# Log-sum-exp kernel: last half tiles with three TensorE-biased heads folded by GpSimd, and two tiles loaded whole

## The chip, the cores and the metric

One core of one Trainium2 chip. The metric is the device time of one execution in microseconds (us). A profile of one execution goes with each kernel; its span is some 2 us shorter than the time, because it runs from the first to the last instruction. Engines in the profile: PE is TensorE's matmuls, PEld its weight loads, DVE is VectorE, ACT ScalarE, POOL GpSimd, SP the engine that issues the loads.

## The reference, cut to what matters

```python
B, S, D, H = 8, 2048, 2048, 8
x_heads = x.reshape(B, S, H, D // H).transpose(0, 2, 1, 3) + bias[None, :, None, :]
x_tiled = np.repeat(x_heads, 2, axis=2)
mx = x_tiled.max(axis=-1, keepdims=True)
lse = mx.squeeze(-1) + np.log(np.exp(x_tiled - mx).sum(axis=-1))
```

For each row and each of 8 heads: the log of the sum over 256 columns of exp(x + bias), each result written twice. The 128 MB input is read once.

## The kernel before

The input comes in 64 tiles of 256 rows (2 MB: 128 partitions, 2 rows, 2048 columns). A head's sum is made in one of four ways:

- TensorE puts the bias in PSUM and adds x by a matmul with the identity ("biased head"); ScalarE takes the exp from PSUM and sums with its accumulator.
- ScalarE takes exp(x) in place and VectorE multiplies by exp(bias) and sums, in one custom instruction ("weighted sum").
- GpSimd adds the bias in SBUF (tiles 0 to 56).
- GpSimd multiplies exp(x) by exp(bias) and halves the head by additions to 32 columns, and VectorE sums these ("fold").

```python
PROMPT_F1 = dict(pe=2, acc=2, g0=8, late=False, fold=1)   # 2 biased heads, 5 weighted, 1 folded
PROMPT_F2 = dict(pe=2, acc=2, g0=8, late=False, fold=2)
SINGLE_F1 = dict(pe=1, acc=1, g0=8, late=False, fold=1)
TRIPLE = dict(pe=3, acc=3, g0=8, late=False, fold=0)
STAGES = [(0, (BULK,)), (54, (MIXED,)),          # whole tiles
    (57, (PROMPT_F1, PROMPT_F1)),                # half tiles from here on
    (62, (SINGLE_F1, SINGLE_F1)), (63, (PROMPT_F2, TRIPLE))]
# ... cut ... the main loop, for one piece (t, k0) of a tile:
            heads = add_x(m, t, k0, c0, c1, bias_here)        # TensorE: x of this half
            if c0 == 0:
                bias_there = put_bias(*next_units.pop(0))     # TensorE: bias of the next half
                keep_warm()                                   # TensorE: three idle matmuls into tp
                flush(for_pool)
            done = exp_inplace(t, ...)                        # ScalarE
            if c0 == 0:
                flush(for_pe)      # ScalarE: biased heads of the half before
            # ... cut ... VectorE: weighted sums
        # ... cut ... after a whole tile, two tiles after a batch's end:
        finish(fb)     # TensorE: four transposes into tp; ScalarE: one Ln of 32x1024 out of tp
```

In the profiles each engine starts its instructions in the order of the program: around tile 57 TensorE starts x of 57.0 at 285.11 us, the next bias at 287.12, the warm matmuls at 287.65, x of 57.1 at 289.09 and the transposes, which the program issues last of these, at 291.91. "Warm matmuls" multiply the identity by itself; nobody reads their result. "57.0" and "57.1" are the two halves of tile 57.

The softmax here doesn't subtract the row's maximum and nothing guards it: scores larger than these inputs give would overflow.

## Time and profile before

| | us |
|---|---|
| time, median of 3 runs | 325.56 (325.21 to 325.87) |
| span of the profiled run | 323.1 |
| half 62.1 lands / ScalarE starts on it | 312.38 / 312.45 |
| ends: GpSimd, ScalarE's sums, VectorE | 319.17, 319.43, 319.63 |

Three lines of the page: busy time and share of each engine, then TensorE's granted clock and the loads in 40 slices of the span, in tenths.

```profile
PE 270.3 (84%) x691; PEld 102.9 (32%) x691; DVE 283.9 (88%) x306; ACT 265.8 (82%) x426; POOL 287.7 (89%) x120
PEclk9979799979979996998997997997999999559998
DMA  8999999999999999999999999999999999999995
```

TensorE (PE), VectorE, ScalarE and GpSimd are each busy for over 80% of the time and the loads keep the DMA engines at eight or nine tenths until the last slice (419 GB/s over the span). No share tells what the end waits for; that is read from the last 36 us, as the prediction does. The two 5s in the clock row are the stretch from 273.6 to 290.6 us in which the clock records have TensorE at half clock; there an x matmul pair takes 2.08 us (at 285.11) and after it 1.02 (at 292.35).

### The profile page before, as it was taken

How to read it: one execution, taken by the hardware profiler on the slowest of the kernel's cores; microseconds unless marked ns; L12 is line 12 of the kernel's file. 1: busy time of each engine (PE TensorE's matmuls, PEld its weight loads, DVE VectorE, ACT ScalarE, POOL GpSimd, SP SyncE). 2: the span in 40 equal slices, each digit the busy share in tenths (PEclk: the TensorE clock that was granted, in tenths of full speed). 3: DMA queues.
4: the chain of work that ended last, by engine and by line, in shares of the span. 5: the costliest groups of instructions: out<-in, count | busy, mean ns of one | idle time of the engine just before them, and what ended most of it. 6: DMA issues, size and time to landing. Idle time of an engine off the chain costs nothing.

```text
span 323.1 us, 2398 instructions
## 1 busy us (share of the span) xinstructions
PE 270.3 (84%) x691; PEld 102.9 (32%) x691; DVE 283.9 (88%) x306; ACT 265.8 (82%) x426; POOL 287.7 (89%) x120
## 2 busy tenths in 40 slices
PE   5999999889978769977869886888997786599984
PEld 2333333333323223322323322333333232035442
DVE  1037779999999998999899899898999999999995
ACT  1148679889869976988888978889998998899995
POOL 6939998999999999999999999999999999858874
PEclk9979799979979996998997997997999999559998
DMA  8999999999999999999999999999999999999995
GB/s 311 457 402 454 450 400 439 450 402 446 438 414 446 432 418 443 430 422 447 422 426 441 422 434 442 404 426 430 432 422 431 430 428 425 416 422 421 419 401 170
DMA packets 8830, 135.42 MB, mean 419 GB/s; under 512 B 1041, under 2 KB 1425, under 8 KB 2417
## 3 DMA queue, kind: packets, MB, share of 16 engines
q1 hardware_dynamic: 8720, 135.27, 98.6%
q8 instruction: 5, 0.08, 0.1%
q14 instruction: 7, 0.06, 0.0%
q10 hardware_dynamic: 98, 0.01, 0.0%
HBM read 134.23 MB, written 1.05 MB: 419 GB/s over the span
## 4 chain that ended last, share of the span: by engine, by line
DMA 40%; POOL 18%; ACT 17%; PE 14%; DVE 9%; issue 0%; SPq 0%; DVEq 0%
DMA xb<-in_x_dram 40%; POOL xb L376 18%; ACT xb L382 11%; DVE R L401 6%; PE pair L326 5%; PE one_ps L326 3%; PE pair L267 3%; ACT xb L357 2%; PE one_ps L267 2%; DVE xb L417 2%; PE pair L219 1%; ACT xb L337 1%; DVE xb L394 1%; ACT res L471 1%; ACT xb L344 1%; DMA brow<-in_bias_dram 1%
## 5 line engine op out<-in xcount | busy, mean ns | idle before, releaser
L376 POOL TENSOR_TENSOR xb<-xb,b_rep 128x2048 f32<-128x2048 f32 x57 | 257.6, 4539 | 20.7 <-DMA xb<-in_x_dram 20.6
L401 DVE TENSOR_REDUCE R<-xb 128x14 f32<-128x3584 f32 (+1 forms) x56 | 214.5, 3830 | 1.9
L382 ACT ACTIVATE xb<-xb 128x2560 f32<-128x2560 f32 (+5 forms) x77 | 157.1, 2050 | 10.3 <-POOL xb L376 10.1
L326 PE MATMUL pair<-xb,ident 128*128 128x512 f32 x216 | 114.3, 656 | 0.0
L326 PE MATMUL one_ps<-xb,ident 128*128 128x512 f32 x108 | 67.5, 710 | 11.5 <-DMA xb<-in_x_dram 11.5
L344 ACT ACTIVATE xb<-pair 128x1024 f32<-128x1024 f32 x54 | 55.5, 1027 | 23.2 <-PE pair L326 23.0
L326 PEld LDWEIGHTS pair<-xb,ident 128*128 128x128 f32 x216 | 46.2, 214 | 61.3 <-issue 61.3
L394 DVE TENSOR_TENSOR xb<-xb,w_ps 128x512 f32<-128x512 f32 x54 | 36.7, 681 | 26.2 <-ACT xb L382 26.2
L337 ACT ACTIVATE xb<-one_ps 128x256 f32<-128x256 f32 x108 | 40.0, 380 | 6.6 <-PE one_ps L326 6.6
L267 PEld LDWEIGHTS <-ones 3*128 3x128 bf16 (+1 forms) x192 | 16.9, 95 | 80.8 <-issue 71.4
L267 PE MATMUL one_ps<-b,ones 3*128 3x512 bf16 x49 | 18.6, 380 | 25.4 <-ACT xb L337 25.3
L267 PE MATMUL pair<-b,ones 3*128 3x512 bf16 x98 | 29.0, 375 | 0.0
L326 PEld LDWEIGHTS one_ps<-xb,ident 128*128 128x128 f32 x108 | 17.2, 200 | 33.9 <-DMA xb<-in_x_dram 18.0
L302 PE MATMUL pair<-xb,ident 128*128 128x512 f32 (+1 forms) x36 | 21.7, 689 | 5.7 <-DMA xb<-in_x_dram 5.7
L417 DVE CUSTOM_DVE_ANT_0 xb<-xb,w_ps 128x256 f32<-128x256 f32 x61 | 22.4, 418 | 0.0
L337 ACT ACTIVATION_READ_ACCUMULATOR xb<-one_ps 128x1 f32 x108 | 22.3, 207 | 0.0
L441 POOL TENSOR_TENSOR xb<-xb 128x128 f32<-128x128 f32 (+3 forms) x39 | 13.8, 355 | 3.1
L433 POOL TENSOR_TENSOR xb<-xb,w_sb 128x256 f32<-128x256 f32 (+1 forms) x13 | 10.0, 771 | 5.2 <-ACT xb L382 4.5
L317 PE MATMUL tp<-ident 128*128 128x128 f32 x84 | 13.7, 302 | 0.0
L317 PEld LDWEIGHTS tp<-ident 128*128 128x128 f32 x84 | 11.1, 200 | 3.5 <-issue 3.0
L357 ACT ACTIVATE xb<-pair 128x256 f32<-128x256 f32 x33 | 11.9, 364 | 0.0
L417 DVE CUSTOM_DVE_ANT_0 xb<-xb,one_ps 128x256 f32<-128x256 f32 x27 | 10.6, 415 | 0.1
(42 smaller groups left out, 83.4 us busy)
## 6 DMA issues: line engine op xcount, KB each, us to landing
xb<-in_x_dram SPq DMA_DIRECT2D x20, 4096.0 KB, 21.5
xb<-in_x_dram SPq DMA_DIRECT2D x17, 2048.0 KB, 22.7
xb<-in_x_dram SPq DMA_DIRECT2D x12, 1024.0 KB, 22.7
xb<-in_x_dram SPq DMA_DIRECT2D x4, 256.0 KB, 13.2
out_dram<-res SPq DMA_DIRECT2D x1, 896.0 KB, 6.7
xb<-in_x_dram SPq DMA_DIRECT2D x2, 384.0 KB, 15.8
xb<-in_x_dram SPq DMA_DIRECT2D x2, 128.0 KB, 6.3
out_dram<-res_last SPq DMA_DIRECT2D x1, 128.0 KB, 1.7
```

The lines of the kernel that those rows point to most:

```text
L267: nc.tensor.matmul(p, lhsT=lhsT, rhs=each_row(b, h * Dh, Dh, K), start=i == 0, stop=False,)
L302: mm = nc.tensor.matmul(p, lhsT=ident, rhs=xts[t % NBUF][:, ka:kb, c : c + w], start=False, stop=True,)
L317: nc.tensor.matmul(tp[:, 0], lhsT=ident, rhs=ident, start=True, stop=True)
L326: mm = nc.tensor.matmul(p, lhsT=ident, rhs=xts[t % NBUF][:, :, h * Dh : (h + 1) * Dh], start=False, stop=True,)
L337: act = nc.scalar.activation(out=xts[t % NBUF][:, k, 0:Dh], in_=got[0][:, k * Dh : (k + 1) * Dh], func=ACT.Exp, accum_out=sums[:, k, 0:1],)
L344: act = nc.scalar.activation(out=xts[t % NBUF][:, :, Dh : m["pe"] * Dh].rearrange("p k (h j) -> p h k j", j=Dh), in_=got[-1].rearrange("p ...
L357: act = nc.scalar.activation(out=xts[t % NBUF][:, k, h * Dh : (h + 1) * Dh], in_=p, func=ACT.Exp, accum_out=sums[:, k, h : h + 1],)
L376: add = nc.gpsimd.tensor_tensor(out=v, in0=v, in1=each_row(b_rep, c - G0, D - c, k1 - k0), op=ALU.add)
L382: return on_x(t, nc.scalar.activation(out=v, in_=v, func=ACT.Exp), [after])
L394: mul = nc.vector.tensor_tensor(out=f, in0=f, in1=each_row(w_ps, m["pe"] * Dh - W0, n, k1 - k0), op=ALU.mult,)
L401: red = nc.vector.tensor_reduce(out=sums[:, k0:k1, h0:H], in_=v.rearrange("p k (h j) -> p k h j", j=Dh), op=ALU.add, axis=mybir.AxisListTy ...
L417: ttr = nc.vector.tensor_tensor_reduce(out=v, in0=v, in1=w, scale=1.0, scalar=0.0, op0=ALU.mult, op1=ALU.add, accum_out=dst,)
```

## The change

Its intent is to take work from VectorE, on which the chain ended, and to save two load instructions. Halves 62.0, 62.1 and 63.0 get three biased heads, of which ScalarE takes one exp from a pair of PSUM banks without summing ("biased exp" below); GpSimd folds all three, without a multiplication. Tiles 57 and 58 are loaded whole. The program gives a three-head unit both banks of a pair, and it puts the next bias after ScalarE's work of the half before, and no longer ahead of the warm matmuls.

```diff
+UNIT_LOADS = 59
-PROMPT_F2 = dict(pe=2, acc=2, g0=8, late=False, fold=2)
-SINGLE_F1 = dict(pe=1, acc=1, g0=8, late=False, fold=1)
+FOLDED = dict(pe=3, acc=0, g0=8, late=False, fold=0)
-    (62, (SINGLE_F1, SINGLE_F1)),
-    (63, (PROMPT_F2, TRIPLE)),
+    (62, (FOLDED, FOLDED)),
+    (63, (FOLDED, TRIPLE)),
-    [(0, 512), (1280, 2048), (512, 1280)],
+    [(0, 768), (1280, 2048), (768, 1280)],
@@ load
+        if t < UNIT_LOADS:
+            ins = nc.sync.dma_start(out=xts[t % NBUF], in_=rows_of(t))
@@ put_bias: a three-head unit starts on a whole pair of banks
+        if n > MM:
+            n_ps[0] += n_ps[0] % 2
@@ new
+    def exp_biased(t, k, n, heads):
+        act = nc.scalar.activation(out=xts[t % NBUF][:, k, 0 : n * Dh],
+            in_=pairs[bank // 2][:, 0 : n * Dh], func=ACT.Exp)
@@ fold: multiplies only heads that carry no bias yet
+        if h0 * Dh >= W1:
@@ main loop
+                    if m["acc"] == 0:
+                        done = exp_biased(t, k, m["pe"], heads)
+                        for_pool.append(fold(t, k, 0, m["pe"], sums, done))
+                        return
-                if next_units and not m["late"]:
-                    bias_there = put_bias(*next_units.pop(0))
-                if t > T_PROMPT and m["g0"] == H:
+                if t > T_PROMPT and m["g0"] == H and m["pe"] * Dh <= MM:
                     keep_warm()
-            if c0 == 0:
+            if c0 == 0 or t == T - 1 and k0 == 0:
                 flush(for_pe)
+            if c0 == 0 and next_units and not m["late"]:
+                bias_there = put_bias(*next_units.pop(0))
```

(Bookkeeping of bank users and of the fold's chain of dependencies is cut.)

More of the change, by code (lines that the diff above doesn't have):

```diff
@@ L166, in load @@
         after = last_uses[t - NBUF] if t >= NBUF else []
+        if t < UNIT_LOADS:
+            ins = nc.sync.dma_start(out=xts[t % NBUF], in_=rows_of(t))
+            on_x(t, ins, after)
+            for k0, _, c0, _ in pieces(t):
+                loads[t, k0, c0] = ins
+            return
         for k0, k1, c0, c1 in pieces(t):
@@ L244, with on_bank @@
     bank_users = [[], []]
-    def on_bank(i, ins):
-        for j, u in bank_users[i // 2]:
-            if j != i and u.ins.engine != ins.ins.engine:
+    def on_bank(i, ins, both=False):
+        pair = i // 2
+        i = None if both else i
+        for j, u in bank_users[pair]:
+            if None not in (i, j) and j != i and u.ins.engine != ins.ins.engine:
                 tc.declare_no_dep(ins.ins, u.ins, reason="another bank")
-        bank_users[i // 2].append((i, ins))
+        bank_users[pair].append((i, ins))
         return ins
@@ L313, in add_x @@
         return heads
+    def exp_biased(t, k, n, heads):
+        _, _, bank, _, mm = heads[-1]
+        act = nc.scalar.activation(
+            out=xts[t % NBUF][:, k, 0 : n * Dh],
+            in_=pairs[bank // 2][:, 0 : n * Dh],
+            func=ACT.Exp,
+        )
+        on_bank(bank, on_x(t, act, [mm]), both=True)
+        return act
     def keep_warm():
@@ L432, in fold @@
         v = xts[t % NBUF][:, k, h0 * Dh : h1 * Dh]
-        done = nc.gpsimd.tensor_tensor(
-            out=v, in0=v, in1=w_sb[:, h0 * Dh - W1 : h1 * Dh - W1], op=ALU.mult
-        )
-        on_x(t, done, [after])
+        done = after
+        if h0 * Dh >= W1:
+            mul = nc.gpsimd.tensor_tensor(
+                out=v, in0=v, in1=w_sb[:, h0 * Dh - W1 : h1 * Dh - W1], op=ALU.mult
+            )
+            done = on_x(t, mul, [done])
         v = v.rearrange("p (h j) -> p h j", j=Dh)
@@ L440, in fold @@
             n //= 2
-            done = nc.gpsimd.tensor_tensor(
+            add = nc.gpsimd.tensor_tensor(
                 out=v[:, :, 0:n], in0=v[:, :, 0:n], in1=v[:, :, n : 2 * n], op=ALU.add
             )
-            on_x(t, done, [])
+            done = on_x(t, add, [done])
         def add_up():
@@ L535, with pe_part @@
                 heads = add_x(m, t, k0, c0, c1, bias_here)
-                def pe_part(t=t, heads=heads, sums=sums):
+                def pe_part(t=t, m=m, k=k0, heads=heads, sums=sums):
+                    if m["acc"] == 0:
+                        done = exp_biased(t, k, m["pe"], heads)
+                        for_pool.append(fold(t, k, 0, m["pe"], sums, done))
+                        return
                     for k, h, bank, p, mm in heads:
```

## The prediction

> **What bounds the kernel now.** I read the page first, then the chain of waits from 286 us on, then the timeline of each engine there; the change touches nothing earlier. The program has 64 tiles of 2 MB; from tile 57 on each is worked on in halves ("57.0", "57.1"). For most of the span the loads bound it: the DMA row shows 9 in every slice but the first and last, 419 GB/s. From 287 us the chain is something else:
>
> ```profile
> 282.59 4.55 POOL xb L376
> 287.17 4.66 ACT xb L382 x3
> 291.82 0.72 ACT xb L357 x4
> 292.55 1.01 ACT res L471
> 293.56 1.38 ACT xb L382
> ...
> 309.53 0.71 ACT xb L357 x4
> 310.24 1.59 ACT xb L382
> 311.83 0.71 ACT xb L357 x4
> 312.54 1.60 ACT xb L382
> 314.16 0.42 DVE xb L417
> 320.11 0.38 ACT res_last L488
> ```
>
> The columns are start, length, engine and line. GpSimd's bias add of tile 56 ends at 287.14, and from there ScalarE works without a gap until the exp of half 62.1 ends at 314.14. Then VectorE takes over: 62.1's six weighted sums, 63.0's four, 63.1's five, at 0.34 each, then a fold's reduce, the transpose, Ln and the store. The timeline of the end:
>
> ```profile
> 312.38 0.70 PE L302 MATMUL pair<-xb,ident 128*128 128x256 f32 x2 [0.72 <-DMA xb<-in_x_dram]
> 312.45 1.68 ACT L382 ACTIVATE xb<-xb 128x1792 f32<-128x1792 f32 x1
> ...
> 317.51 1.66 POOL L441 TENSOR_TENSOR xb<-xb 128x256 f32<-128x256 f32 x3
> ...
> 319.25 0.18 ACT L357 ACTIVATION_READ_ACCUMULATOR xb<-pair 128x1 f32 x1
> ...
> 319.41 0.22 DVE L447 TENSOR_REDUCE R_last<-xb 128x2 f32<-128x64 f32 x1
> ```
>
> The reader is to see that half 62.1 lands at 312.38 and ScalarE gets to it at 312.45, so ScalarE has just caught up with the loads and has nothing in hand; and that all three tail engines end close together: GpSimd 319.17, ScalarE 319.43, VectorE 319.63. The rest (319.63 to 323.1) is fixed. So a delay of ScalarE after 287 us, or a later end of any one of the three, moves the time almost one for one.
>
> [...] 128x128 takes 457 ns, 128x256 730 ns, 2.13 ns per element. [...] the same 512-column x matmul pair takes 2.08 us at 285.11 and 1.02 us at 292.35, and the clock records give half clock from 273.6 to 290.7. [...]
>
> **The change part by part.**
>
> *Loads.* Tiles 57 and 58 come as one 2 MB load each. In the trace halves land 2.485 us apart and whole tiles 4.90, so two tiles save 2 x (4.97 - 4.90) = 0.15 us of loading: 62.1 lands at 312.23. But 57.0 is no longer there at 285.11; the tile lands whole at about 282.59 + 4.86 = 287.45. ScalarE doesn't mind, since it exps 57.0 at 288.9 and 58.0 at 293.5. TensorE does:
>
> ```profile
> 285.11 2.08 PE L302 MATMUL pair<-xb,ident 128*128 128x512 f32 x2
> 287.12 0.60 PE L284 MATMUL pair<-b,ones 3*128 3x512 bf16 x1
> 287.65 1.65 PE L317 MATMUL tp<-ident 128*128 128x128 f32 x6
> 289.09 1.80 PE L302 MATMUL pair<-xb,ident 128*128 128x512 f32 x2
> 290.82 0.38 PE L284 MATMUL pair<-b,ones 3*128 3x512 bf16 x1
> 291.14 0.94 PE L317 MATMUL tp<-ident 128*128 128x128 f32 x6
> 291.91 0.60 PE L461 MATMUL tp<-ident,R 128*32 128x128 f32 x4
> ```
>
> This queue is in order, and its last row is the transpose that ScalarE's Ln of the first seven batches (292.55, in the chain) waits for. In the changed program it still stands behind both halves of tile 57 (the order of the bias and the warm matmuls is swapped, which costs nothing by itself). From 287.45: x of 57.0 at half clock 2.0, warm matmuls 1.25, bias 0.35, weights and x of 57.1 at full clock 1.2, warm 0.75, bias 0.3, transposes 0.7: done at 294.0 against 292.5. ScalarE then stalls about 1.4 us in front of its Ln. [...]
>
> *ScalarE in the tail.* Back to back a 1536 exp takes a step of 1.37 and a 1792 exp 1.59, 0.21 per 256 columns; so 1280 takes 1.16, and 768 takes 0.73 (826 ns, overlapping by 0.1). A PSUM source costs the same (1024 columns, 1.03 us). Tiles 62 and 63.0 lose four one-head exps with their accumulator reads (0.355 each) and gain three 768 exps from PSUM, while the exps in place shrink by 512, 512 and 256 columns. The sum of ScalarE's work falls from 8.57 to 8.3 us: no lever either way.
>
> *VectorE.* Halves 62.0 and 62.1 go from six to five weighted sums, 63.0 from four to five: one less, -0.34; three reduces of 96 instead of 32, 32 and 64 elements give back about 0.2.
>
> *GpSimd.* It loses the multiplications (0.73, 0.73 and 1.27 us) and folds three heads of each of 62.0, 62.1, 63.0. At 2.13 ns per element 384, 192 and 96 elements take 1.00 + 0.59 + 0.39 us, plus two gaps of 0.08: 2.14 each, 6.43 for three, against 1.92 + 1.92 + 3.0 before. The sum is slightly smaller, but it starts later. Before, the fold of 62.0 began at 311.91, right after the exp of its last heads. Now it needs the exp of the biased heads of 62.0, and in the changed order that stands behind 62.0's other exp, 61.1's two heads and the exp of 62.1, which waits for its load.
>
> *The sum.* Let A be the start of the exp of 62.1. The biased exp of 62.0 ends at A + 1.16 + 0.72 + 0.10, GpSimd starts at A + 2.04 and ends its third fold at A + 8.47, and the last reduce (0.25) ends at A + 8.75. On the other engines: TensorE's bias and x for 63.0 need the pair that 62.0 had, about 2.0 us (bias 0.5, weights, 512 and 256 columns 1.45) after A + 1.98, so ScalarE's biased exp of 63.0 starts at A + 4.0 and ScalarE ends at A + 7.85; VectorE, held up by the reduce of 62.0's fold, comes out at A + 8.15. GpSimd ends last by some 0.3 us. Without the stall, A is 312.23 + 0.07 = 312.30 and the last reduce ends at 321.05, 1.42 later than 319.63. With a stall of 1.4, A is 310.15 + 1.4 + 1.16 + 0.71 = 313.42, and the end is 2.54 later. So the working gives 325.56 + 1.4 = 327.0 to 325.56 + 2.5 = 328.1. I choose 327.4: [...] a tuned change is more likely to have a delay that I overrate than one that I miss.
>
> **The rivals.**
>
> *It gains.* The intent is to drain VectorE, on which the chain ends. If VectorE alone set the end, and the biased exps came as promptly as before, one weighted sum less and loads 0.15 us earlier make 325.1. For it: VectorE is busy from 314.16 to the end. Against it: GpSimd and ScalarE end within 0.5 us of it, so they take its place at once.
>
> *Only the tail counts, no Ln stall.* If TensorE's clock rises early, or the transposes come sooner, the time is 327.0. [...]
>
> *The clock stays low longer.* With 57.0 late TensorE idles from 285.2 to 287.4; [...]
>
> *The early loads matter.* Fewer loads could shorten everything by 0.15 us. But ScalarE, not the loads, is the chain from 287 to 314; it is hidden.
>
> **Range and chances.** The rival with a gain and the worked sum with the stall span 325.1 to 328.1, the slow clock adds a tail above. The range is 325.4 to 328.9. All these lie within 2% (319.0 to 332.1): faster by over 2% would need 6.5 us from a tail of 36 us whose loads alone end at 317.6; slower by over 2% would need the slow clock and a second delay.
>
> **What would show it.** Right: an idle time of ScalarE of 0.6 to 1.5 us in front of L471's successor, ended by TensorE's transpose; three GpSimd folds of about 2.1 us each, back to back, the first starting near 314.3 to 315.5; a last reduce on VectorE that waits for GpSimd; a wait of about 0.5 us of ScalarE for TensorE before the biased exp of 63.0. Wrong: a fold of three heads well under 2 us, GpSimd done before VectorE, or ScalarE passing the Ln without a gap and starting 62.0 at 310.15 or earlier.

Gone are two other sizes of the stall: a smaller one, for an earlier rise of the clock, which was the 0.6 us in "0.6 to 1.5 us" (an estimate of the author without working), and a larger one, for a later rise, on which the part of the range above 328.1 rests; and with them what was said for and against these two clock rivals. For the larger one the trace gives a size: the half-clock stretch from 222.41 to 225.82 us lasts 3.41; were the one before the Ln longer by as much, TensorE would be behind by half of that, 1.7 us, the stall some 3.1 and the time some 329.8 (an estimate from these numbers).

## The result, and the profile after

The changed kernel takes 328.76 us (median of 4, 328.04 to 328.99) against 325.38 (median of 4) before. The ratio is 1.0098, 95% interval 1.0078 to 1.0118: slower by 1%, within the 2% of "same". A ratio here and below is the mean time of one kernel's fast runs over that of the other's fast runs of the same rounds, so not quite the ratio of the medians. Executions over 1.5% slower than the fastest of the same kernel are left out of the means.

The page of the changed kernel, busy times and clock row:

```profile
PE 267.4 (82%) x676; PEld 102.0 (31%) x676; DVE 284.6 (87%) x304; ACT 265.8 (82%) x421; POOL 287.6 (88%) x117
PEclk9989799979979987997999997997999997569997
```

GpSimd's and ScalarE's busy sums moved by 0.1 us or less and VectorE's by 0.7, while the span grew by 2.9. So hardly any work was added; it was moved and made to wait. The chain of waits that ended last is followed back from the last instruction, at each step to what released it. In order of time (start, length, engine, buffer and line; line 314 is the x matmul, 340 the warm matmuls, 296 the bias, 486 the transposes, 496 the Ln, 405 the exp in place, 330 the biased exp, 466 a fold's addition, 472 the reduce that ends a fold):

```profile
287.54 2.08 PE pair L314 x2
289.62 1.28 PE tp L340 x6
290.90 0.34 PE pair L296
291.24 1.06 PE pair L314 x2
292.29 0.67 PE tp L340 x6
292.96 0.32 PE pair L296
293.27 0.56 PE tp L486 x4
...
293.85 1.01 ACT res L496
...
313.44 1.16 ACT xb L405
314.60 0.70 ACT xb L330
...
315.37 1.01 POOL xb L466
...
321.98 0.27 DVE R_last L472
```

Before, this stretch was ScalarE from 287 to 314 and VectorE after that. Now TensorE stands at its head, GpSimd at its end. The two hand-overs, in the timelines of ScalarE and GpSimd; the bracket is the idle time just before and what ended it:

```profile
293.85 1.01 ACT L496 ACTIVATE res<-tp 32x1024 f32<-32x1024 f32 x1 [1.31 <-PE tp L486]
```

```profile
315.37 6.57 POOL L466 TENSOR_TENSOR xb<-xb 128x384 f32<-128x384 f32 x9 [2.44 <-ACT xb L330]
```

Before, GpSimd's first instruction for 62.0 was

```profile
311.91 0.73 POOL L433 TENSOR_TENSOR xb<-xb,w_sb 128x256 f32<-128x256 f32 x1 [0.31 <-ACT xb L382]
```

ScalarE reaches the Ln of the seventh batch and waits 1.31 us for the transposes. GpSimd, with nothing to do for 2.44 us, starts its first three-head fold at 315.37 and ends its third at 321.94. The last reduce ends at 322.23, where it ended at 319.63.

### The profile page after: what moved, and what is told of

Its sections match the earlier page's. It is cut to its first block, busy times and chain, and to the rows that moved or that the text cites. A ratio compares the mean times of both kernels' runs of the same rounds, so it can differ in the third digit from the quotient of the medians.

```text
span 326.0 us, 2354 instructions
## 1 busy us (share of the span) xinstructions
PE 267.4 (82%) x676; PEld 102.0 (31%) x676; DVE 284.6 (87%) x304; ACT 265.8 (82%) x421; POOL 287.6 (88%) x117
## 3 DMA queue, kind: packets, MB, share of 16 engines
HBM read 134.23 MB, written 1.05 MB: 415 GB/s over the span
## 4 chain that ended last, share of the span: by engine, by line
DMA 40%; POOL 20%; ACT 16%; PE 15%; DVE 7%; issue 1%; POOLq 0%; SPq 0%
DMA xb<-in_x_dram 40%; POOL xb L399 18%; ACT xb L405 10%; DVE R L424 6%; PE pair L349 4%; PE pair L277 3%; PE one_ps L349 2%; ACT xb L380 2%; POOL xb L466 2%; PE one_ps L277 2%; ACT xb L360 2%; PE pair L226 1%; DVE xb L417 1%; PE pair L314 1%; ACT xb L367 1%; ACT res L496 1%
## 5 line engine op out<-in xcount | busy, mean ns | idle before, releaser
L349 PEld LDWEIGHTS pair<-xb,ident 128*128 128x128 f32 x216 | 45.9, 213 | 60.8 <-issue 60.8
L314 PE MATMUL pair<-xb,ident 128*128 128x512 f32 (+1 forms) x42 | 23.6, 662 | 6.7 <-DMA xb<-in_x_dram 6.7
L277 PE MATMUL pair<-b,ones 3*128 3x512 bf16 x98 | 28.8, 373 | 0.0
L466 POOL TENSOR_TENSOR xb<-xb 128x128 f32<-128x128 f32 (+5 forms) x39 | 16.4, 423 | 5.3 <-ACT xb L330 2.4
L458 POOL TENSOR_TENSOR xb<-xb,w_sb 128x256 f32<-128x256 f32 x10 | 7.3, 732 | 5.9 <-ACT xb L405 5.2
L314 PEld LDWEIGHTS pair<-xb,ident 128*128 128x128 f32 x42 | 7.2, 206 | 16.9 <-DMA xb<-in_x_dram 10.6
L496 ACT ACTIVATE res<-tp 32x1024 f32<-32x1024 f32 x7 | 7.1, 1013 | 5.4 <-PE tp L486 5.4
L340 PEld LDWEIGHTS tp<-ident 128*128 128x128 f32 x60 | 8.9, 206 | 5.9 <-issue 4.9
L380 ACT ACTIVATE xb<-pair 128x256 f32<-128x256 f32 x29 | 10.5, 368 | 0.0
```

What stands on the lines that cost most here:

```text
L277: nc.tensor.matmul(p, lhsT=lhsT, rhs=each_row(b, h * Dh, Dh, K), start=i == 0, stop=False,)
L314: mm = nc.tensor.matmul(p, lhsT=ident, rhs=xts[t % NBUF][:, ka:kb, c : c + w], start=False, stop=True,)
L349: mm = nc.tensor.matmul(p, lhsT=ident, rhs=xts[t % NBUF][:, :, h * Dh : (h + 1) * Dh], start=False, stop=True,)
L380: act = nc.scalar.activation(out=xts[t % NBUF][:, k, h * Dh : (h + 1) * Dh], in_=p, func=ACT.Exp, accum_out=sums[:, k, h : h + 1],)
L466: add = nc.gpsimd.tensor_tensor(out=v[:, :, 0:n], in0=v[:, :, 0:n], in1=v[:, :, n : 2 * n], op=ALU.add)
```

## The experiments

Theory: two separate losses. (1) Tile 57 loaded whole comes late for TensorE, whose transposes for the Ln stand behind it. (2) The folds of the three biased heads start late, and GpSimd ends last. Rivals: the loads are hidden, or are the whole loss; the tail is the whole loss; ScalarE or VectorE sets the end anyway. All kernels below gave correct results. The kernel before, run beside them, had medians of 325.27 to 325.29.

| run | median us (runs) | ratio to before | idle before the Ln, in the profile |
|---|---|---|---|
| e1_loads_only | 328.10 (5) | 1.0080 | 2.73 |
| e2_tail_only | 326.81 (5) | 1.0048 | none |
| e3_ln_later | 328.28 (4) | 1.0092 | 1.01 |
| e4_biased_first | 327.68 (5) | 1.0073 | 1.69 |
| e5_no_third_fold | 327.34 (6) | 1.0060 | 2.32 |
| e6_transposes_first | 326.95 (5) | 1.0047 | none |
| e7_warm_before | 327.08 (5) | 1.0050 | 0.64 |
| e8_first_and_first | 326.19 (6) | 1.0025 | none |
| e9_factor_in_psum | 328.27 (5) | 1.0086 | 1.60 |
| e10_all_three | 325.97 (5) | 1.0015 | none |
| e11_changed_again | 328.50 (4) | 1.0090 | 1.83 |

**The loads alone.** The kernel before with

```diff
+        if t < 59:
+            ins = nc.sync.dma_start(out=xts[t % NBUF], in_=rows_of(t))
```

> The kernel before with nothing changed but the loads: tiles 57 and 58 whole. If the late arrival of half 57.0 holds TensorE's queue and with it the transposes in front of ScalarE's Ln (my theory), ScalarE shows an idle time of 1.0 to 1.5 us in front of that Ln and the time is 326.4 to 327.1, about 1.2 us over before. If whole loads are hidden or help (rival), it is 325.1 to 325.6. If they are the whole loss (rival), it is 328.5 or more.

It cost 2.8 us, more than twice what I expected. ScalarE's timeline:

```profile
295.19 1.01 ACT L479 ACTIVATE res<-tp 32x1024 f32<-32x1024 f32 x1 [2.73 <-PE tp L469]
```

The place is the one predicted; the size is not. In this profile the clock rose only at 293.7 by the clock records (290.9 in the changed kernel), so x of 57.1 took 1.91 us in place of about 1.1, and here the bias of 57.1 runs ahead of the warm matmuls. The clock fell again at 317.6, and TensorE at half clock stands in this run's chain at its end, so the 2.8 us are not quite the wait alone. Two whole loads can thus cost nearly as much as the whole change.

**The tail alone.** The changed kernel with

```diff
-UNIT_LOADS = 59
+UNIT_LOADS = 57
```

> The changed kernel with tiles 57 and 58 loaded in halves again, so only the tail and the order of bias and warm matmuls are changed. My theory: ScalarE passes the Ln without a gap, the exp of 62.1 starts near 312.4, GpSimd's three folds start near 314.4 and end near 321, and the time is 326.8 to 327.6, some 1.2 to 1.8 us over before. Rival that the loads are the whole loss: 325.2 to 325.6. Rival that the tail is the whole loss: 328.5 or more.

326.81 us, as expected. ScalarE has no gap at the Ln, catches up with the loads, and GpSimd still starts late:

```profile
312.25 1.27 ACT L405 ACTIVATE xb<-xb 128x1280 f32<-128x1280 f32 x1 [0.41 <-DMA xb<-in_x_dram]
```

```profile
314.30 6.57 POOL L466 TENSOR_TENSOR xb<-xb 128x384 f32<-128x384 f32 x9 [2.98 <-ACT xb L330]
```

So neither part is the whole loss. The two single losses, 2.8 and 1.5 us, add up to more than the 3.2 to 3.4 of the change. In this tail the first 0.4 us of a delay fall into ScalarE's wait for 62.1. The rest of the difference may come from the other order of bias and warm matmuls in e1 and from its later clock; no run separates these.

**The Ln one tile later.** Transposes and Ln after tile 58:

```diff
-        fb, at = divmod(t - 2, NBLK)
+        fb, at = divmod(t - (3 if t > T_PROMPT else 2), NBLK)
```

> The changed kernel, whole loads kept, with the transposes and the Ln of the first seven batches issued one tile later (after tile 58 in place of 57). If the whole loads cost through this Ln alone, the idle time in front of it is under 0.2 us and the time falls by 1.0 to 1.4 us from the changed kernel, to about that of the run with the tail alone, 326.8 to 327.6. If whole loads cost in another way (57.0's other work late, slower transfers), it stays at 328.3 to 329.

A miss: the time stayed at 328.28. The wait moved along with the Ln:

```profile
298.07 1.01 ACT L496 ACTIVATE res<-tp 32x1024 f32<-32x1024 f32 x1 [1.01 <-PE tp L486]
```

I had thought that TensorE would be back on time by then. But its chain in this profile repeats 1.05 (x), 0.67 (warm) and 0.32 (bias) us for each half: 2.04, beside ScalarE's 1.37 + 0.71 = 2.08. TensorE gains 0.04 us a half and stays late. The biased exps don't notice (ScalarE has no idle time before them here), because TensorE works one half ahead of them; the Ln has no such lead, wherever it stands behind the queue.

**The transposes first.** They go right behind 57.0's warm matmuls; those of 57.1 are dropped, since they write the same PSUM:

```diff
+                    if (t, k0) != (57, 1):
                         keep_warm()
+                if (t, k0) == (57, 0):
+                    turn(B - 2)      # the four transposes, taken out of finish()
```

> The changed kernel, whole loads kept, Ln kept in its place on ScalarE, but the four transposes it reads come right behind half 57.0 on TensorE, and 57.1's warm matmuls are dropped (they would overwrite the transposes). The run with the Ln one tile later kept its wait, and I now read that as TensorE staying late: its unit takes 2.04 us beside ScalarE's 2.085, so it never catches up. If the place in TensorE's queue is what costs, the idle time in front of the Ln is under 0.3 us and the time is that of the tail alone, 326.6 to 327.3. If whole loads cost otherwise, it stays at 328.0 to 328.8.

326.95 us, the time of the tail alone, with the loads still whole:

```profile
292.55 1.00 ACT L501 ACTIVATE res<-tp 32x1024 f32<-32x1024 f32 x1
```

No idle time. Its five runs lie within 0.08 us (326.90 to 326.98), where eight runs of the changed kernel, over two sessions, spread from 327.80 to 328.99. So the Ln's wait is the loss by the whole loads, to within the 0.14 us between this run and e2. It is a part of what makes the changed kernel's time unsteady (see the second profile below), but not all: e2 and e8, without that wait, spread over 0.7 and 1.1 us. The run moves the transposes and drops three warm matmuls in one; which of them did how much it does not tell.

**Six warm matmuls ahead of 57.0.**

```diff
+                if (t, k0) == (57, 0):
+                    for _ in range(2):
+                        keep_warm()
                 heads = add_x(m, t, k0, c0, c1, bias_here)
```

> The changed kernel with six more warm matmuls in front of half 57.0, in the time in which TensorE waits for the whole tile (285.2 to 287.4). If the low clock is a part of the wait in front of the Ln, TensorE comes to full clock by 288 or so, the idle time falls from 1.3 to 2 us to about 0.6 us, and the time from 328.8 to 327.6 to 328.1. If the clock has no part in it, or does not rise earlier, it stays at 328.2 to 329.0.

327.08 us, below the expected 327.6 to 328.1, and all five runs lie below all eight of the changed kernel. The clock rose at 289.3 and not by 288, which was the author's estimate, and the wait shrank as expected:

```profile
293.21 1.01 ACT L496 ACTIVATE res<-tp 32x1024 f32<-32x1024 f32 x1 [0.64 <-PE tp L486]
```

More work on TensorE made the kernel 1.4 us faster than the changed kernel's second session. The clock is a part of the loss, as a cause.

**The changed kernel again, unaltered.**

> The changed kernel unaltered, for its spread and for a second profile. Its four first times lay at 328.04 and at 328.7 to 329.0, and I take this for TensorE's clock: in the runs so far that keep its order at tile 57, the idle time in front of the Ln grew from 0.64 to 1.31, 1.69 and 2.32 us as the clock rose at 289.3, 290.9, 291.8 and 293.0, about 0.5 us per us. So this profile should lie on that line: an idle time of 1.31 + 0.47 x (rise - 290.9) us, within 0.15. The median should be 328.0 to 329.0. Rival: the spread comes from elsewhere, and the profile is off the line.

The clock rose at 292.0 and the idle time was 1.83 us; the line gives 1.81. Six profiles keep this order behind 57.0, and by the rise of the clock their waits are: e7 0.64 us at 289.3, the changed kernel 1.31 at 290.9, e9 1.60 at 291.5, e4 1.69 at 291.8, this run 1.83 at 292.0, e5 2.32 at 293.0. All lie within 0.1 us of the line; four of them had been used to draw it, e9 and this run had not. A slope of about a half is what the half clock would give (in the chain of the changed kernel an x matmul pair takes 2.08 us before the rise and 1.06 after it): each us that the rise comes later, TensorE does half a us less work. Where the rise falls differs from run to run of the same program (290.9 and 292.0).

**The biased exp of 62.0 first.** ScalarE takes it ahead of the exp of 62.1; the order on the other engines stays.

```diff
+            elif heads and m["acc"] == 0 and t < T - 1:
+                pe_part()
+                add_up = for_pool.pop()
+                for_pe.append(lambda f=add_up: for_pool.append(f))
```

> The changed kernel with one pair of ScalarE instructions swapped: the biased exp of half 62.0 comes before the exp of 62.1 in place of after it. If GpSimd's late start sets the end, its first fold starts about 1.1 us earlier (near 314.3 with the Ln stall still there), its third ends near 320.9, and the end comes 0.8 to 1.1 us earlier, time 327.5 to 328.0. Rival that ScalarE or VectorE sets the end: no gain or a loss, 328.5 to 329.2, since the exp of 62.1 comes 0.7 us later.

327.68 us, 0.8 to 1.1 less than the two sessions of the changed kernel. GpSimd:

```profile
314.70 6.64 POOL L466 TENSOR_TENSOR xb<-xb 128x384 f32<-128x384 f32 x9 [1.37 <-ACT xb L330]
```

This profile had 0.38 us more of the Ln's wait than the first one of the changed kernel (1.69 against 1.31), and yet the folds start 0.67 earlier; they end at 321.34. The late start did set the end. But the gain stops there: in this chain of waits VectorE runs to 322.09, so it ends last again.

**No third fold.** ScalarE sums the three heads of 63.0 itself.

```diff
-    (63, (FOLDED, TRIPLE)),
+    (63, (TRIPLE, TRIPLE)),
```

> The changed kernel with the fold of half 63.0 taken away: ScalarE sums its three heads itself (0.36 us each in place of one exp of 0.70). If GpSimd's third fold sets the end, GpSimd ends 2.2 us earlier and no longer last, ScalarE ends about 0.4 us later than in the changed kernel (near 321.5) and sets the end with VectorE, and the time falls by 0.5 to 0.9 us, to 327.9 to 328.2. Rival that ScalarE or VectorE sets the end already: the time rises by up to 0.4 us, 328.8 to 329.2.

327.34 us, 1.2 below the changed kernel's second session and more than I expected; the sign decides for GpSimd. In its profile two folds end at 320.73, VectorE's last reduce at 322.39, with 1.0 us more of the Ln's wait than in the first profile of the changed kernel. So the third fold costs more than its absence costs ScalarE.

**Both repairs.** The edits of e6 and e4 together.

> Both repairs in the changed kernel: transposes right behind half 57.0, and the biased exp of 62.0 before the exp of 62.1. If the two losses are separate and add up, each repair gives what it gives alone: about 1.6 us and 0.9 us off 328.8, so 325.6 to 326.5, still not under the kernel before, since ScalarE's biased exp of 63.0 still waits for TensorE and VectorE takes over as the last engine. If they are one loss seen twice, it stays near 327.3.

326.19 us. From the second session's 328.50 the repairs take 1.55 and 0.82 alone and 2.31 together, against a sum of 2.37: two losses that add up, as far as runs that spread over 1.1 us can tell.

**Head 7's factor in PSUM.** In the changed kernel VectorE's last weighted sum took 0.85 us, the others 0.42:

```profile
320.50 0.42 DVE L440 CUSTOM_DVE_ANT_0 xb<-xb,w_ps 128x256 f32<-128x256 f32 x1
320.85 0.85 DVE L440 CUSTOM_DVE_ANT_0 xb<-xb,w_sb 128x256 f32<-128x256 f32 x1
```

Its factor `w_sb` lies in SBUF, those of the other heads (`w_ps`) in PSUM. A GpSimd addition ran from 320.83 to 321.42. The edit:

```diff
+                nc.vector.tensor_copy(one_ps[:, 0:Dh], w_sb[:, Dh : 2 * Dh])   # at t == 62
-        if c < W0:
+        if h == H - 1 and t >= 62:
+            w = one_ps[:, 0:Dh]
+        elif c < W0:
```

> The changed kernel with the factor of head 7 copied to PSUM for tiles 62 and 63, so that VectorE's weighted sum of that head has one input in SBUF in place of two. In the changed kernel the last one took 0.85 us beside a GpSimd add, where the others take 0.42. If the two engines hold each other up over SBUF there, all four take under 0.45 us beside GpSimd, GpSimd's adds of 192 elements take about 0.60 us in place of 0.66 and 0.72, and its last fold ends 0.1 to 0.2 us earlier; the time moves by no more than that, since GpSimd ends last. Rival that the 0.85 is something else: it stays.

GpSimd's additions in the tail, grouped by shape (busy us and mean ns), first of the changed kernel, then of this run:

```profile
L466 POOL TENSOR_TENSOR xb<-xb 128x384 f32<-128x384 f32 x3 | 3.0, 1001 | 2.4 <-ACT xb L330 2.4
L466 POOL TENSOR_TENSOR xb<-xb 128x192 f32<-128x192 f32 x3 | 2.0, 655 | 0.2
L466 POOL TENSOR_TENSOR xb<-xb 128x96 f32<-128x96 f32 x3 | 1.2, 407 | 0.2
```

```profile
L468 POOL TENSOR_TENSOR xb<-xb 128x192 f32<-128x192 f32 x3 | 1.8, 594 | 0.2
L468 POOL TENSOR_TENSOR xb<-xb 128x96 f32<-128x96 f32 x3 | 1.2, 386 | 0.2
```

And VectorE's sums with the copied factor in this run:

```profile
L442 DVE CUSTOM_DVE_ANT_0 xb<-xb,one_ps 128x256 f32<-128x256 f32 x4 | 1.7, 416 | 0.0
```

As expected: the four sums take 0.42 us on average, three of them beside GpSimd, and the three folds take 6.32 us in place of 6.57. The time hardly moved (328.27). With the factor in SBUF, in the changed kernel, the three sums that overlap an addition of 192 elements took 0.51, 0.42 and 0.85 us and those additions 0.66, 0.72 and 0.59; with it in PSUM, here, the four sums took 0.42 and the additions 0.59 on average. So the place of this factor cost both engines time; by what mechanism, these runs do not show.

**All three.** The edits of e6, e4 and e9.

> Transposes first, biased exp of 62.0 first, and the factor of head 7 in PSUM. The run with the first two gave 326.19 us, with VectorE and ScalarE last. VectorE held one sum of head 7 up there too. I expect 325.8 to 326.2, 0 to 0.3 us under that run: a version that equals the kernel before at best. If it came under 325.0 it would beat both.

325.97 us: 0.2 under e8, as expected, 0.7 over the kernel before, and the ratio's interval (1.0001 to 1.0029) leaves almost no room for a tie. Its chain of waits is VectorE without a gap from before 305 us to 320.24, with the added copy (0.34) in it. In this profile and in e8's, VectorE has no gap at all from the reduce of tile 56 to the end. From the start of that reduce it needed 28.8 us in e8 (two sums of head 7 took 1.16 and 0.85 us beside GpSimd) and 27.9 here; but it started it at 291.33 in e8 and at 292.31 here. In all profiles this start lies between 290.4 and 292.3, a spread that arises before the edited tiles and whose cause is not shown. With both waits repaired it reaches the end, so two single profiles don't size the third repair. No version beat the kernel before.

## Why the prediction was right, and where it was off

The range (325.4 to 328.9) and the class hold; the point, 327.4, was 1.4 us under the measured median. Step by step, against the profile of the changed kernel:

- *Loads: TensorE's transposes end at 294.0, ScalarE stalls about 1.4.* They ended at 293.83 and the stall was 1.31. e6 shows that this is the whole cost of the loads, within 0.14 us. (The Ln that waits is the seventh batch's alone, not that of seven batches, as the prediction says; the sum doesn't depend on it.) What I had not seen is that TensorE makes up only 0.04 us a half (e3).
- *ScalarE is no lever, VectorE has one sum less.* Busy time of ScalarE unchanged (265.8 in both). VectorE waited 0.94 us for the first fold.
- *A = 313.42, GpSimd starts at A + 2.04, three folds take 6.43, last reduce ends at 322.17.* Measured: the exp of 62.1 at 313.44 in the chain, folds from 315.37, 6.57 long, reduce ended at 322.23. The folds took 0.14 more than the sum; the 0.25 us that e9's edit took off them (6.57 to 6.32) are a term that the sum lacked, so without it the folds were charged 0.11 too much. The wait of ScalarE for TensorE before the biased exp of 63.0 was 0.37 us (about 0.5 was expected), with 0.20 more before that of 62.1.
- *The rest after the reduce is fixed.* Not quite: 3.8 us in place of 3.5. The final transpose took 0.45 us and not 0.30, and the clock records have TensorE at half clock from 321.6 on. In the kernel before they show the drop at 321.4, after its transpose was done.
- *VectorE at A + 8.15, GpSimd last by some 0.3.* It was GpSimd, but VectorE waited only 0.1 us for it: its reduce before ended at 321.87, the last one began at 321.98. So when GpSimd's start was repaired (e4), VectorE took over as the last and the gain stopped at 0.8 to 1.1 us.
- *I choose 327.4.* This is the step that failed. The working gave 328.1 with the stall, and I shaded it down because I held it likelier that I overrate a delay than that I miss one. Neither delay was overrated: the stall came, at 1.31 and 1.83 us, and GpSimd ended last. The stall was sized for one time of the clock's rise; its usual size is probably nearer to 1.8 (the second profile) than to 1.4, since six of the changed kernel's eight times lie 0.4 us or more above the 328.04 of the run that had 1.31. That the range holds is in part luck: the median lies 0.14 us under its upper end, and one run of 328.99 above it.
- *TensorE's clock: half from 273.6 to 290.7.* The two speeds hold; what makes the clock rise no run shows. Before the rise at 290.64 TensorE's matmuls stood without a gap from 282.57, 8.1 us. Four profiles of programs that are the same up to the rise (the changed kernel twice, e3, e5) have it between 290.8 and 293.0, 2.2 us apart, though TensorE starts on tile 57 within 0.32 us (287.47 to 287.79).

Of the rivals, "it gains" is refuted by e2 and e5; "only the tail counts" is what e6 builds, and its time of 326.95 is the 327.0 given there; "the clock stays low longer" was real in part: the rise came as late as 293.0 (e5) and 293.7 (e1), with waits of 2.32 and 2.73 us. "The early loads matter" doesn't show: the load of 62.1 released its exp at 312.25 with half loads (e2) and at 312.44 with whole ones (e6).

## What to carry to other kernels

When a load is merged, ask not only whether its data come in time for the engine that sets the pace, but what stands behind their first use in the queue of each engine, which in these profiles starts its work in program order; here a transposing step for another batch did. Moving work to a less busy engine helped here only as far as its input was ready early (GpSimd idle for 2.44 us before the first fold, and 0.8 to 1.1 us gained in e4 by starting it sooner): look at when the new producer's result comes, in the producer's own order, and count the moved work from there. An engine whose period nearly equals that of the pacing engine (here 2.04 and 2.08 us) hardly makes up for a delay, so put what others wait for ahead of its filler work.
